# State space constants on VectorE in pieces, and half of the block product's weight sums by adding transfers

## The chip, the cores and the metric

The kernel runs on one core of a Trainium2 chip. The core has TensorE (PE: matmuls, 128 rows by up to 512 columns), VectorE (DVE) and ScalarE (ACT) for elementwise work, GpSimd (POOL), SyncE (SP) and DMA queues that SP, ACT and POOL issue to. Each engine runs its own list of instructions in order and waits for the others by semaphores. The metric is the device time of one execution in microseconds (us); lower is better.

## The reference

One layer of a hybrid decoder block on x of 512 tokens by 1024 features, all in float32:

```python
h = h + 0.5 * swiglu(rmsnorm(h, norm_ffn1), ffn1_w1, ffn1_w3, ffn1_w2)   # d_ff 2816
z = rmsnorm(h, norm_mix) @ w_in           # attention q, k, v, gates, and u for S5
h = h + concat([o_nsa, o_s5]) @ w_out
h = h + 0.5 * swiglu(rmsnorm(h, norm_ffn2), ffn2_w1, ffn2_w3, ffn2_w2)
h = h + sigmoid(rmsnorm(h, norm_ple) @ w_ple_gate) * (p @ w_ple)
out = rmsnorm(h, norm_final)

def swiglu(x, w1, w3, w2):
    return (silu(x @ w1) * (x @ w3)) @ w2
```

The S5 mixer is a diagonal complex state space model of 32 groups with 64 states, 16 channels in and out. The kernel computes it with matrices built from the parameters: powers of the discretised transition (`pr`, `pi`) times the input and output matrices, and a table of cosines and sines of the state's angles (`tcs`). These constants depend on no token.

## The kernel before

**Layout and stages.** The activations lie transposed in SBUF as `h`, 128 partitions by 8 blocks by 512 tokens. In order run the first FFN (to some 412 us of the profile), the mixer (to 700), the second FFN (to 1062), and the gate and the last norm.

**Products.** All weights come as units of 128x1024 floats (512 KB), loaded into `raw`, a ring of four buffers (`load_unit`, L104 to 109). The loads are issued on ACT's queue. `split` (L142 to 150) makes two halves of reduced precision: ACT casts `hi` (L147), DVE subtracts `lo` (L149). Each product is three matmuls, hi by hi, hi by lo and lo by hi.

**FFN.** d_ff is cut into 22 tiles f of 128, in chunks 0-5, 6-11, 12-16, 17-21. `FFN_ORDER` makes the up product of the first tile of a chunk, then the down product of the chunk before it, then the other up tiles. A down product has 8 steps m; each is 18 (or 15) matmuls of 512 columns into `ps_C`, and DVE adds the result to `h` (L470).

An up tile f below `plain` takes 48 matmuls of 512 columns. The others are fast tiles: a block scheme of 7 products on quarters of the weights and of x (`begin`, `up_fast`), 84 matmuls of 256 columns in all. It needs sums of quarters of the weights. `prepare` makes them on two raw units r0 and r1, in place: four DVE operations of 128x512 (L344, L346, L347, L350), between which the units are split, and at last the split of the fourth sum into `ah` (ACT, L352) and `al` (DVE, L353). x's own combinations are made by `restate`, with four 128x1024 operations on POOL (L216 to L225). `plain` is 5 in the first FFN and 2 in the second.

**S5 constants.** `s5_constants` is a generator that the first FFN draws from. After an up tile f it is advanced as its yielded numbers say. DVE makes the small tables, POOL the large ones: `ft` (L670 to 672), `gt` (L687 to 689), `tcs` (L741 to 748). So that POOL does not start early, each block is issued after a small copy `seen` on POOL of a copy `step` on DVE from the tile just made (L503, L457). `turn_f` transposes `ft` on PE and stores `fs`; `make_m` makes `kt` on PE and stores it by 8 small transfers on SP's queue (L709), and `gt` by three. `fs`, `kt` and the table `w` share one buffer ("bx").

**Order.** A scheduler places each engine's instructions from the code's order and its own estimate of times; the buffers of the pools limit how far ahead it can put a load.

Of the kernel before, what the change touches and what calls it, by code (L numbers as in the profile page):

```python
# [76 lines left out]
def block_kernel(ctx: ExitStack, tc: tile.TileContext, a: dict, out: bass.AP):  # L77
# [53 lines left out]
    def unit(raw_only=False, keep=None, q=nc.scalar, after=None):  # L131
# [3 lines left out]
        if i not in raws:  # L135
            load_unit(i, q)
# [24 lines left out]
    class Norm:  # L161
# [34 lines left out]
        def restate(self, xs, t, pool):  # L196

            def row(k):
                return xs[k // 4][:, k % 4]

            def quarter(r, c):
                return xs[r][:, :, 256 * c:256 * c + 256]
# [8 lines left out]
            self.row = row  # L211
            for k in range(KT):
                V.scalar_tensor_tensor(row(k), h[:, k, :], gains[:, self.gi, k:k + 1], self.rb, OP.mult, OP.mult)  # L213
# [5 lines left out]
            G.tensor_tensor(t, t, quarter(1, 1), OP.subtract)  # L219
            yield  # L220
            self.t2 = held(2)
            G.tensor_tensor(t, t, quarter(1, 0), OP.add)
            yield
            self.t4 = held(4)
            G.tensor_tensor(quarter(0, 1), quarter(0, 1), quarter(1, 1), OP.subtract)  # L225
# [3 lines left out]
        def resplit(self, k):  # L229
            S.copy(self.xh[:, k], self.row(k))  # L230
            V.tensor_tensor(self.xl[:, k], self.row(k), self.xh[:, k].bitcast(F32), OP.subtract)

# [91 lines left out]
    def ffn(nrm, done, plain, xp, hp, fp, bg=None, first=None, restate=None):  # L324
        wait = next(bg) if bg else None
        fast = not bg
        if True:
            hid = {}

            def hidden(f, t3):  # L330
                hq = hp.tile([128, 2, SEQ], FR, tag="hq", name="hq")
                hh, hl = hq[:, 0], hq[:, 1]
                if fast or f >= plain:
                    S.copy(hh, t3)  # L334
                else:
                    V.tensor_copy(hh, t3)
# [3 lines left out]
            def prepare(f):  # L340

                r0, r1 = unit(True), unit(True)
                a0, a1 = (r.rearrange("p (b c) -> p b c", b=2) for r in (r0, r1))
                V.tensor_tensor(a0[:, 1], a0[:, 0], a0[:, 1], OP.add)  # L344
# [5 lines left out]
                V.tensor_tensor(a1[:, 1], a0[:, 1], a1[:, 1], OP.add)  # L350
# [38 lines left out]
            def up_fast(f, after):  # L389
# [12 lines left out]
                t1 = fp.tile([128, SEQ], F32, tag="t1", name="t1")  # L402
# [14 lines left out]
            def up(f):  # L417
# [21 lines left out]
                t1 = fp.tile([128, SEQ], F32, tag="t1", name="t1")  # L439
# [14 lines left out]
            def step(f):  # L454
                if bg and wait is not None:
                    state["step"] = pace.tile([128, 1], F32, tag="step", name="step", bufs=3)
                    V.tensor_copy(state["step"], hid[f][1][:, 0:1].bitcast(F32))  # L457

            def down(fl, last):
                n = len(fl)  # L460
                cur = None
                for m in range(KT):
# [7 lines left out]
                    V.scalar_tensor_tensor(h[:, m, :], o, 0.5, h[:, m, :], OP.mult, OP.add)  # L470
                    if last:
                        done(m)
                    elif m == KT - 2:
                        for _ in begin(fl[-1] + 2):
                            pass

            for kind, i in FFN_ORDER:
                if kind == "up":
                    up(i)
                    step(i)  # L480
                    for _ in range(4):
                        if wait is not None and i >= wait:
                            wait = next(bg, None)
# [13 lines left out]
    def s5_constants(sp):  # L497
        yield 6
        if True:
            def paced():  # L500

                seen = sp.tile([128, 1], F32, tag="seen", name="seen")
                return tc.issue_after(G.tensor_copy(seen, state["step"]).ins)  # L503

# [3 lines left out]
            def late(dst, src):  # L508
                with tc.issue_after(loads[7].ins):
                    nc.scalar.dma_start(dst, src)  # L510
# [43 lines left out]
            yield 1  # L554
# [6 lines left out]
            yield 1  # L561

            J = 9
# [4 lines left out]
            for j in range(1, J):  # L568
                V.tensor_scalar(ph[:, j], ph[:, 0], float(2 ** j), None, OP.mult)
            yield 1  # L570
# [7 lines left out]
            yield 1  # L578
# [5 lines left out]
            yield 1  # L584
# [5 lines left out]
            yield 1  # L590

            pr, pi = t32("pr", 9), t32("pi", 9)
            u1, u2 = t32("u1", 4), t32("u2", 4)
# [16 lines left out]
            yield 1  # L610
# [15 lines left out]
            yield 1  # L626
# [16 lines left out]
            yield 1  # L643
# [19 lines left out]
            def big(c, n, name):  # L663
                t = sp.tile([128, 8, n, 16], F32, tag=f"big{c % 2}", name=name)
                return t, sp.tile([128, 8, n, 16], F32, tag="bt", name="bt")

            def make_f(c):
                ft, bt = fts[c], _ = big(c, 8, "ft")
                with paced():
                    G.tensor_tensor(*spread(ft, b2[:, 0, chunk(c)], pr[:, 0:8, chunk(c)]))  # L670
                    G.tensor_tensor(*spread(bt, b2[:, 1, chunk(c)], pi[:, 0:8, chunk(c)]))
                    G.tensor_tensor(ft, ft, bt, OP.add)
# [11 lines left out]
            def make_g(c):  # L684
                gt, bt = gts[c], _ = big(c, 9, "gt")
                with paced():
                    G.tensor_tensor(*spread(gt, cx[:, 0, chunk(c)], pr[:, :, chunk(c)]))  # L687
                    G.tensor_tensor(*spread(bt, cx[:, 1, chunk(c)], pi[:, :, chunk(c)]))
                    G.tensor_tensor(gt, gt, bt, OP.subtract)
# [4 lines left out]

            def make_m(c):
                kt = sp.tile([16, 8, 128], F32, tag="bx", name="kt")
                p = bank("C")
                for n in range(8):
                    j, i = n // 4, n % 4
                    mm(p[32 * j:32 * j + 16, i * 128:(i + 1) * 128], b2[:, 0, 8 * c + n, :],  # L700
                       gts[c][:, n, 0:8].rearrange("p k o -> p (k o)"), True, True)
# [10 lines left out]
            for i in range(10):  # L712
                yield 7 + i
# [894 lines left out]
```

## Time and profile before

| | us |
|---|---|
| median of 3 runs | 1123.72 |
| lowest, highest | 1117.9, 1126.02 |
| the profiled execution | 1124.48 |
| its span | 1122.7 |
| mean clock of PE granted | 0.978 of full speed |
| busy POOL in the span | 180.1 |

The profile is of one execution, of which 1.8 us lie outside the span. Its views used below: the page's shares and the chain that ended last (followed back from the last instruction to what released it); busy times by stretch of the span; the groups of instructions of a line and shape with their count, total and mean; the chain of waits in a stretch in order of time; and the transfers with their size and the median time from issue to landing. PE's matmuls overlap in the records, so the mean length of a record is longer than the time between two.

### The profile page before, as it was taken

The page shows a single profiled execution, that of the slowest core. Times are in us where ns is not written, and L with a number is a line of the kernel's source. Part 1 is how long each engine was busy: PE and PEld are TensorE (multiplying, and loading weights), DVE is VectorE, ACT ScalarE, POOL GpSimd, SP SyncE. Part 2 cuts the span into 40 slices and gives each one's busy share as a digit, 9 for nine tenths or more (in the row PEclk, how much of TensorE's full clock was granted, in tenths as well). Part 3 has the DMA queues.
Part 4 walks back from the last instruction along what each step waited for, and adds up shares of the span by engine and source line. Part 5 has one row for each costly group of instructions (what it writes and reads, how often), then busy time and mean ns, then how long its engine had stood idle before and what let it go on. Part 6 is the DMA issues. An engine that isn't in the chain of part 4 may idle for free.

```text
span 1122.7 us, 16766 instructions
## 1 busy us (share of the span) xinstructions
PE 1054.2 (94%) x6518; PEld 908.0 (81%) x6518; DVE 847.6 (75%) x1362; ACT 518.3 (46%) x918; POOL 180.1 (16%) x174
## 2 busy tenths in 40 slices
PE   6989997999899899989799999999999999999996
PEld 5778897889789778867457667699899899898895
DVE  6899889868657796689548896887578658666776
ACT  5344253425424442345736894655245335245541
POOL 5210027623432982010000000000000000000000
PEclk9999998999999999999989999999999999999998
DMA  8314222643632557885522002324323313324402
GB/s 257 117 38 151 75 76 88 209 116 86 182 95 76 169 138 243 231 264 155 178 85 76 1 20 71 135 76 123 104 75 114 132 57 113 132 76 151 148 22 75
DMA packets 76543, 132.78 MB, mean 118 GB/s; under 512 B 26528, under 2 KB 45984, under 8 KB 76464
## 3 DMA queue, kind: packets, MB, share of 16 engines
q10 hardware_dynamic: 26080, 90.51, 25.7%
q1 hardware_dynamic: 47312, 29.89, 9.6%
q0 software_dynamic: 3072, 11.31, 3.1%
q8 instruction: 51, 0.84, 0.3%
q14 instruction: 28, 0.23, 0.1%
HBM read 114.09 MB, written 17.83 MB: 118 GB/s over the span
## 4 chain that ended last, share of the span: by engine, by line
PE 70%; DVE 12%; issue 6%; ACT 6%; DMA 4%; SPq 1%; ACTq 0%; DVEq 0%; POOLq 0%; POOL 0%
PE ps_C L126 22%; PE ps_B L126 19%; PE ps_A L126 19%; PE ps_D L126 11%; DVE lo L149 4%; DMA raw<-in_wpack 2%; DMA qf<-qd 1%; ACT e L850 1%; ACT hi L147 1%; SPq L709 1%; ACT eh L850 1%; ACT ps_B L850 1%; DVE t L414 1%; DVE xn L213 1%; DVE hq L337 1%
## 5 line engine op out<-in xcount | busy, mean ns | idle before, releaser
L149 DVE TENSOR_TENSOR lo<-raw,hi 128x1024 fp32r<-128x1024 f32 (+2 forms) x203 | 270.4, 1358 | 70.8 <-ACT hi L147 68.7
L147 ACT CAST hi<-raw 128x1024 fp32r<-128x1024 f32 (+2 forms) x203 | 207.6, 1041 | 244.3 <-PE ps_C L126 91.7
L126 PE MATMUL ps_C<-hq,hi 128*128 128x512 f32 x704 | 219.2, 393 | 4.0 <-ACT hq L334 2.3
L126 PEld LDWEIGHTS ps_C<-hq,hi 128*128 128x128 f32 x704 | 131.0, 189 | 33.4 <-DVE h L470 3.2
L126 PE MATMUL ps_A<-xh,lo 128*128 128x256 f32 (+1 forms) x456 | 140.3, 308 | 7.1 <-DVE lo L149 7.1
L126 PE MATMUL ps_A<-xh,hi 128*128 128x256 f32 (+1 forms) x456 | 139.8, 309 | 7.1 <-ACT xh L170 6.4
L126 PE MATMUL ps_A<-xl,hi 128*128 128x256 f32 (+1 forms) x456 | 140.9, 311 | 2.5 <-DVE xl L171 1.1
L126 PE MATMUL ps_C<-hq,lo 128*128 128x512 f32 x352 | 136.6, 391 | 0.0
L302 POOL TENSOR_TENSOR ri<-ms,negh 128x4 f32<-128x4 f32 (+1 forms) x6 | 7.4, 1226 | 589.6 <-DVE ms L301 589.5
L126 PEld LDWEIGHTS ps_A<-xh,lo 128*128 128x128 f32 x456 | 87.2, 191 | 11.8 <-DVE lo L149 8.2
L126 PEld LDWEIGHTS ps_A<-xh,hi 128*128 128x128 f32 x456 | 87.0, 192 | 11.7 <-ACT xh L170 6.4
L126 PEld LDWEIGHTS ps_A<-xl,hi 128*128 128x128 f32 x456 | 87.0, 192 | 11.1 <-DVE xl L171 3.9
L126 PE MATMUL ps_B<-sh,hi 128*128 128x256 f32 x296 | 86.5, 292 | 7.1 <-ACT pu L365 4.9
L126 PE MATMUL ps_B<-sl,hi 128*128 128x256 f32 x296 | 85.4, 288 | 0.0
L126 PE MATMUL ps_B<-sh,lo 128*128 128x256 f32 x296 | 85.0, 287 | 0.0
L126 PEld LDWEIGHTS ps_C<-hq,lo 128*128 128x128 f32 x352 | 66.4, 189 | 13.8
L126 PE MATMUL ps_D<-sh,lo 128*128 128x256 f32 x228 | 64.2, 282 | 2.2 <-DVE lo L149 2.2
L126 PEld LDWEIGHTS ps_B<-sh,hi 128*128 128x128 f32 x296 | 58.2, 197 | 9.4 <-ACT pu L365 5.5
L126 PE MATMUL ps_D<-sh,hi 128*128 128x256 f32 x228 | 63.9, 282 | 0.4 <-ACT hi L147 0.4
L126 PE MATMUL ps_D<-sl,hi 128*128 128x256 f32 x228 | 63.6, 281 | 0.0
L126 PEld LDWEIGHTS ps_B<-sl,hi 128*128 128x128 f32 x296 | 58.2, 196 | 0.2
L126 PEld LDWEIGHTS ps_B<-sh,lo 128*128 128x128 f32 x296 | 58.3, 197 | 0.0
(407 smaller groups left out, 2469.0 us busy)
## 6 DMA issues: line engine op xcount, KB each, us to landing
raw<-in_wpack ACTq DMA_DIRECT2D x168, 512.0 KB, 3.7
so<-s5o POOLq DMA_DIRECT2D x8, 768.0 KB, 6.3
si<-s5i POOLq DMA_DIRECT2D x8, 512.0 KB, 6.6
raw<-in_wpack SPq DMA_DIRECT2D x4, 512.0 KB, 6.6
h<-in_xT SPq DMA_DIRECT2D x8, 256.0 KB, 5.3
s5i<-fs SPq DMA_DIRECT2D x4, 512.0 KB, 3.9
s5o<-gt SPq DMA_DIRECT2D x4, 512.0 KB, 3.3
s5o<-gt SPq DMA_DIRECT2D x8, 256.0 KB, 4.6
```

The costliest lines, as they stand in the source:

```text
L126: return PE.matmul(o, lhsT, rhs, start=start, stop=stop, **kw)
L147: S.copy(hi[:, c], raw[:, c])
L149: V.tensor_tensor(lo[:, c], raw[:, c], hi[:, c].bitcast(F32), OP.subtract)
L213: V.scalar_tensor_tensor(row(k), h[:, k, :], gains[:, self.gi, k:k + 1], self.rb, OP.mult, OP.mult)
L302: G.tensor_tensor(ri, ms, negh[:, :nb], OP.pow)
L337: V.tensor_tensor(hl, t3, hh.bitcast(F32), OP.subtract)
L414: V.tensor_tensor(t3, t1, t3, OP.mult)
L709: nc.sync.dma_start(md[16 * (7 - e):16 * (7 - e) + 16, chunk(c), 16 * e:], kt[:, :, :128 - 16 * e])
L850: S.activation(*args, **kw)
```

## The change

**S5 constants.** `ft`, `gt` and `tcs` are made by DVE. `rotated` makes each of `ft` and `gt` in three operations and yields after each; `tcs` is rewritten as four operations on both halves at a time for each doubling, where six were. `step`, `seen` and `paced` are gone. The new `aside(n, mark)` advances the generator n times, with the pieces issued after the instruction `mark`: behind the h-update of each step of a down product (2 pieces for even m, 1 for odd m, in the first chunk from m = 5), three pieces after the up tiles 4, 5 and 6, and one after each from 8 on.

**Weight sums.** In `prepare` the first sum is an accumulating transfer on POOL's queue that reads the quarter again from DRAM (L362 of the new kernel), and the fourth one from SBUF to SBUF (L368). Each moves 128x512 floats. The second and third sum stay on DVE (L364, L365).

**Raw units.** While `more` is set, every fifth unit in the first FFN lies in a fifth buffer, and in the second FFN there are eight; the loads go to SP's queue, not ACT's.

**Others.** `PLAIN1` is 7, not 5. `restate` runs on DVE, in 128x512 pieces, and its input lies in other buffers (`Rows`). `hidden` always copies on ACT. `t1` has one buffer in the first FFN. S5 parameters are loaded on SP's queue.

```diff
+    more = []
     def load_unit(i, q):
         w = UNIT_W[i]
-        raw = ring.tile([128, UNIT], F32, tag="raw", name="raw", bufs=4)
+        if more and i % (4 + more[1]) >= 4:
+            raw = more[0].tile([128, UNIT], F32, tag="raw", name="raw", bufs=more[1])
+        else:
+            raw = ring.tile([128, UNIT], F32, tag="raw", name="raw", bufs=4)
...
         if i not in raws:
-            load_unit(i, q)
+            load_unit(i, q or (nc.sync if more else nc.scalar))
...
-            G.tensor_tensor(t, quarter(0, 1), quarter(0, 0), OP.subtract)
+            combine(tq, quarter(0, 1), quarter(0, 0), OP.subtract)
...
             def prepare(f):
+                i = unit_i[0]
                 r0, r1 = unit(True), unit(True)
                 a0, a1 = (r.rearrange("p (b c) -> p b c", b=2) for r in (r0, r1))
-                V.tensor_tensor(a0[:, 1], a0[:, 0], a0[:, 1], OP.add)
+                src = a["wpack"][128 * UNIT_OFF[i]:128 * UNIT_OFF[i + 1]].rearrange("(p c) -> p c", c=UNIT)
+                nc.gpsimd.dma_start(a0[:, 1], src[:, 0:512], accum_op=OP.add)
                 yield split(r0)
                 V.tensor_tensor(a0[:, 1], a0[:, 1], a1[:, 0], OP.add)
                 V.tensor_tensor(a0[:, 0], a0[:, 0], a0[:, 1], OP.subtract)
                 yield split(r0)
                 yield split(r1)
-                V.tensor_tensor(a1[:, 1], a0[:, 1], a1[:, 1], OP.add)
+                nc.gpsimd.dma_start(a1[:, 1], a0[:, 1], accum_op=OP.add)
...
-            def step(f):
-                if bg and wait is not None:
-                    state["step"] = pace.tile([128, 1], F32, tag="step", name="step", bufs=3)
-                    V.tensor_copy(state["step"], hid[f][1][:, 0:1].bitcast(F32))
+            def aside(n, mark=None):
+                for _ in range(n if bg else 0):
+                    with tc.issue_after(mark.ins) if mark else nullcontext():
+                        next(bg, None)
...
-                    V.scalar_tensor_tensor(h[:, m, :], o, 0.5, h[:, m, :], OP.mult, OP.add)
+                    mark = V.scalar_tensor_tensor(h[:, m, :], o, 0.5, h[:, m, :], OP.mult, OP.add)
...
+                    if not last:
+                        aside((2 - m % 2) * (m > 4 or fl[0] > 0), mark)
...
                     up(i)
-                    step(i)
-                    for _ in range(4):
-                        if wait is not None and i >= wait:
-                            wait = next(bg, None)
+                    aside(SMALL.get(i, int(i > 7)))
...
-            def make_f(c):
-                ft, bt = fts[c], _ = big(c, 8, "ft")
-                with paced():
-                    G.tensor_tensor(*spread(ft, b2[:, 0, chunk(c)], pr[:, 0:8, chunk(c)]))
-                    G.tensor_tensor(*spread(bt, b2[:, 1, chunk(c)], pi[:, 0:8, chunk(c)]))
-                    G.tensor_tensor(ft, ft, bt, OP.add)
+            def rotated(kept, c, n, name, x, y, sub):
+                t = kept[c] = sp.tile([128, 8, n, 16], F32, tag=f"big{c % 2}", name=name)
+                u = sp.tile([128, 8, n, 16], F32, tag="bt", name="bt")
+                V.tensor_tensor(*spread(t, x[:, chunk(c)], pr[:, 0:n, chunk(c)]))
+                yield
+                V.tensor_tensor(*spread(u, y[:, chunk(c)], pi[:, 0:n, chunk(c)]))
+                yield
+                V.tensor_tensor(t, t, u, sub)
+                yield
...
-                        G.tensor_tensor(t, si, bi, OP.mult)
-                        G.tensor_tensor(dr, sr, br, OP.mult)
-                        G.tensor_tensor(dr, dr, t, OP.subtract)
-                        G.tensor_tensor(t, si, br, OP.mult)
-                        G.tensor_tensor(di, sr, bi, OP.mult)
-                        G.tensor_tensor(di, di, t, OP.add)
+                    V.tensor_tensor(t[:, 0], old[:, 1], angle(nsn, 1), OP.mult)
+                    V.tensor_tensor(t[:, 1], old[:, 0], angle(sn, 1), OP.mult)
+                    V.tensor_tensor(new, old, angle(cs, 2), OP.mult)
+                    V.tensor_tensor(new, new, t, OP.add)
...
+    more[:] = fp2, 4
     ffn(n2, feed_next(3), N_PLAIN, x2pool, hp2, fp2)
+    del more[:]
...
-PLAIN1 = 5
+PLAIN1 = 7
+SMALL = {4: 3, 5: 3, 6: 3}
```

**How the order of instructions moves.** First DVE in the second FFN, one steady fast tile, before (t: the tile's product, p and pu: copies of partial sums):

```order
L149 TENSOR_TENSOR lo<-raw,hi 128x1024 x3
L350 TENSOR_TENSOR raw<-raw 128x512
L414 TENSOR_TENSOR t_7996<-t_7995,t_7996 128x512
L346 TENSOR_TENSOR raw<-raw 128x512
L353 TENSOR_TENSOR al<-raw,ah 128x512
L404 TENSOR_TENSOR t_8121<-ps_D,pu 128x256
L347 TENSOR_TENSOR raw<-raw 128x512
L337 TENSOR_TENSOR hq<-t_7996,hq 128x512
L344 TENSOR_TENSOR raw<-raw 128x512
L408 TENSOR_TENSOR t_8121<-p_8065,ps_B 128x256
```

The same cycle of DVE after:

```order
L154 TENSOR_TENSOR lo<-raw,hi 128x1024 x3
L432 TENSOR_TENSOR t_7661<-t_7660,t_7661 128x512
L364 TENSOR_TENSOR raw<-raw 128x512
L365 TENSOR_TENSOR raw<-raw 128x512
L353 TENSOR_TENSOR hq<-t_7661,hq 128x512
L422 TENSOR_TENSOR t_7786<-ps_D,pu 128x256
L371 TENSOR_TENSOR al<-raw,ah 128x512
L426 TENSOR_TENSOR t_7786<-p_7730,ps_B 128x256
```

Two of the four sums are gone from the cycle (L344 and L350 before); `al` (L371) now reads what the transfer of L368 has written.

In the first FFN POOL's list before, in the middle of the constants:

```order
L503 COPY seen<-step 128x1
L687 TENSOR_TENSOR gt<-cx,pr 128x1152
L688 TENSOR_TENSOR bt<-cx,pi 128x1152
L689 TENSOR_TENSOR gt<-gt,bt 128x1152
L503 COPY seen<-step 128x1
```

DVE's list after, where the second down product begins (h is its update):

```order
L488 SCALAR_TENSOR_TENSOR h<-ps_C,h 128x512
L678 TENSOR_TENSOR ft<-b_862,pr 128x1024
L680 TENSOR_TENSOR bt<-b_862,pi 128x1024
L432 TENSOR_TENSOR t_1824<-t_1823,t_1824 128x512
L154 TENSOR_TENSOR lo<-raw,hi 128x1024
L353 TENSOR_TENSOR hq<-t_1824,hq 128x512
L488 SCALAR_TENSOR_TENSOR h<-ps_C,h 128x512
L682 TENSOR_TENSOR ft<-ft,bt 128x1024
```

The products have left POOL and stand between DVE's updates of h, one or two behind each.

POOL at the end of the mixer and the start of the second FFN, after (L908 loads an S5 constant, L322 is the norm's power):

```order
L908 DMA so<-s5o 128x1536 x2
L362 DMA raw<-in_wpack 128x512 x2
L322 TENSOR_TENSOR ri<-ms,negh 128x4
L362 DMA raw<-in_wpack 128x512 x2
L368 DMA raw<-raw 128x512
```

Before, the power (L302) stood right behind the last load of S5; now two adding transfers stand between them.

SP's queue in the first FFN, after:

```order
L714 DMA s5o<-kt 16x8x16
L111 DMA raw<-in_wpack 128x1024
L698 DMA s5o<-gt 128x8x128
L700 DMA s5o<-gt 64x8x128 x2
L111 DMA raw<-in_wpack 128x1024
L698 DMA s5o<-gt 128x8x128
L700 DMA s5o<-gt 64x8x128 x2
L714 DMA s5o<-kt 16x8x128
```

The loads of weights, which stood on ACT's queue, now stand between the stores of `gt` and `kt`.

More of the change, by code (lines that the diff above doesn't have):

```diff
@@ L194, in quarter, with restate @@
             return self.xh[:, ks, cs], self.xl[:, ks, cs]
[L196 to L202, printed above, removed]
+        def restate(self, rows, t, pool):
+            self.row = lambda k: rows[k]
             def held(n):
@@ L231, in resplit, with __init__, pair, __getitem__ @@
             V.tensor_tensor(self.xl[:, k], self.row(k), self.xh[:, k].bitcast(F32), OP.subtract)
+    class Rows:
+        def __init__(self, tiles):
+            self.pairs = [tiles[0][:, 0:2], tiles[0][:, 2:4], *tiles[1:]]
+        def pair(self, k):
+            return self.pairs[k // 2]
+        def __getitem__(self, k):
+            return self.pairs[k // 2][:, k % 2]
     class Scaled(Norm):
@@ L332, in hidden @@
                 hh, hl = hq[:, 0], hq[:, 1]
[L333 to L336, printed above, removed]
+                S.copy(hh, t3)
                 V.tensor_tensor(hl, t3, hh.bitcast(F32), OP.subtract)
@@ L438, in up @@
                     nrm.finish()
[L439 removed]
+                t1 = fp.tile([128, SEQ], F32, tag="t1", name="t1", bufs=2 if fast else 1)
                 t3 = fp.tile([128, SEQ], F32, tag="t3", name="t3")
@@ L682, in turn_f, with make_m @@
                 nc.sync.dma_start(fd[:, chunk(c)], fs)
[L684 to L689, printed above, removed]
+            def make_m(c):
+                gt = gts[c]
                 ko = gt[:, :, 1:9, :].rearrange("p g k o -> p g (k o)")
@@ L711, in s5_constants @@
             fts, gts = {}, {}
-            for i in range(10):
-                yield 7 + i
-                if 2 <= i < 6:
-                    turn_f(i - 2)
-                if i >= 6:
-                    make_m(i - 6)
-                if i < 4:
-                    make_f(i)
-                elif i < 8:
-                    make_g(i - 4)
+            late_ = []
+            for kept, n, name, x, y, sub, then in ((fts, 8, "ft", b2[:, 0], b2[:, 1], OP.add, turn_f),
+                                                   (gts, 9, "gt", cx[:, 0], cx[:, 1], OP.subtract, make_m)):
+                for c in range(4):
+                    for i, _ in enumerate(rotated(kept, c, n, name, x, y, sub)):
+                        if i == 1 and late_:
+                            late_.pop()()
+                        yield
+                    late_.append(lambda then=then, c=c: then(c))
@@ L747, in s5_constants, with angle @@
-                nc.sync.dma_start(cd[:, gs_], tc_)
-                G.tensor_scalar(ts_, ts_, pos, None, OP.mult)
-                nc.sync.dma_start(sd[:, gs_], ts_)
+                    def angle(t, m):
+                        t = t[:, 1 + j, gs_]
+                        if m > 1:
+                            return t[:, None, :, None].to_broadcast([128, m, 16, n])
+                        return t[:, :, None].to_broadcast([128, 16, n])
+                    old, new, t = tcs[:, :, :, 0:n], tcs[:, :, :, n:2 * n], w1[:, :, :, 0:n]
@@ L752, in block_kernel @@
+                V.tensor_scalar(tcs[:, 1], tcs[:, 1], pos, None, OP.mult)
+                nc.sync.dma_start(sd[:, gs_], tcs[:, 1])
+                yield
     state = {}
@@ L767, in block_kernel @@
         bg = s5_constants(sp)
-        xs = [sp.tile([128, 4, SEQ], F32, tag=f"big{i}", name="xn") for i in range(2)]
         xt = sp.tile([128, 4, 256], F32, tag="bt", name="xt")
-        for k in range(KT):
-            n1.square(k, G, xs[k // 4][:, k % 4])
         with (tc.tile_pool(name="xpool1", bufs=1, reuse_waits="tile") as x1,
@@ L774, in block_kernel @@
             pad(x1, XSHIFT)
-            parts = n1.restate(xs, xt, x1)
             with tc.tile_pool(name="hid", bufs=7, reuse_waits="tile") as hp1:
                 hp1.tile([128, (512 - XSHIFT) // 4], F32, name="pad", bufs=1)
-                ffn(n1, feed_next(1), PLAIN1, x1, hp1, fp1, bg, first, parts)
+                rows = Rows([sp.tile([128, 4, SEQ], F32, tag="big0", name="xn")] +
+                            [hp1.tile([128, 2, SEQ], F32, tag="hq", name="xn") for _ in range(2)])
+                for k in range(KT):
+                    n1.square(k, G, rows[k])
+                more[:] = fp1, 1
+                ffn(n1, feed_next(1), PLAIN1, x1, hp1, fp1, bg, first, n1.restate(rows, xt, x1))
+                del more[:]
         for _ in bg:
```

88 lines of the change are left out of this document (44 added, 44 removed).

## The prediction

> **What bounds the kernel now.** I read the page first, from the top. TensorE (PE) is busy 94% of the span, and the chain that ended last is 70% PE. So nearly three quarters of the time is matmul, and what a change of this kind can win is the rest of that chain: VectorE (DVE) 12%, ACT 6%, issue 6%, DMA 4%.
>
> ```profile
> span 1122.7 us, 16766 instructions
> PE 1054.2 (94%) x6518; PEld 908.0 (81%) x6518; DVE 847.6 (75%) x1362; ACT 518.3 (46%) x918; POOL 180.1 (16%) x174
> PE 70%; DVE 12%; issue 6%; ACT 6%; DMA 4%; SPq 1%; ACTq 0%; DVEq 0%; POOLq 0%; POOL 0%
> ```
>
> Shares are means over unlike stages, so I cut the span into stretches next: the first FFN (to 412 us), the mixer (412 to 700), the second FFN (700 to 1062), the rest. The columns are the stretch, its length, busy time of PE, its weight loads, DVE, ACT and GpSimd (POOL), then clock, DMA share, GB/s.
>
> ```profile
> 60.00:106.00 46.00, 41.56 (x249) 36.59 (x248) 45.73 (x108) 22.29 (x34) 2.40 (x1) 0.96 0.28 88
> 142.00:210.00 68.00, 58.53 (x450) 57.25 (x449) 61.65 (x62) 33.53 (x60) 34.58 (x18) 0.92 0.33 102
> 260.00:310.00 50.00, 43.84 (x348) 40.44 (x348) 37.05 (x51) 24.18 (x42) 23.05 (x12) 0.96 0.56 158
> 370.00:412.00 42.00, 37.36 (x191) 31.14 (x190) 35.39 (x37) 18.27 (x29) 40.70 (x50) 0.96 0.56 162
> 700.00:742.00 42.00, 39.44 (x193) 31.28 (x192) 35.20 (x53) 24.66 (x35) 1.03 (x1) 1.00 0.31 102
> 742.00:1030.00 288.00, 288.00 (x2046) 271.05 (x2045) 203.08 (x273) 129.66 (x210) 0.00 (x0) 1.00 0.34 106
> ```
>
> The last row is the yardstick. From 742 to 1030 PE never stops, and POOL does nothing. In the first FFN the same tiles run, but POOL is at work for the S5 constants, and PE has holes in exactly the stretches where POOL is busy: 142 to 210, 260 to 310, 370 to 412.
>
> What an unbroken PE does is in the chain of waits of the second FFN (start, length, what, number of instructions): a down product's 512-column matmul takes 23.14/102 = 0.227 us. A fast up tile starts its like piece at 845.32 and again at 855.25, so a tile lasts 9.93 us; its 84 matmuls of 256 columns take 0.118 us each.
>
> ```profile
> 791.81 23.14 PE ps_C L126 x102
> 845.32 1.91 PE ps_A L126 x16
> 855.25 1.91 PE ps_A L126 x16
> ```
>
> Now the stretch of the first FFN from 106.2 us (end of the first plain tiles) to 412, 305.8 us. The groups of PE by shape there:
>
> ```profile
> L126 PE MATMUL ps_C<-hq,hi 128*128 128x512 f32 x324 | 102.2, 396 | 2.5 <-ACT hq L334 1.2 <-DVE h L470 0.9 <-ACT fs L681 0.3
> L126 PE MATMUL ps_C<-hq,lo 128*128 128x512 f32 x163 | 63.8, 393 | 0.0
> L126 PE MATMUL ps_B<-sh,hi 128*128 128x256 f32 x120 | 36.6, 305 | 4.9 <-ACT pu L365 4.9
> L126 PE MATMUL ps_C<-gt,b 128*16 128x128 f32 x64 | 6.9, 274 | 0.7 <-POOL gt L689 0.7
> ```
>
> There are 324 + 163 = 487 down matmuls: 110.6 us. The 120 of the third row are 8 in each of 15 fast tiles (f = 7 to 21): 15 x 9.93 = 149.0 us. The S5 products are the 64 of the last row and 32 transposes, about 10 us. That makes 270 of 305.8, so some 35 us are lost there. By the same count with a cut at each stretch I get 15.5 us lost from 142 to 210, 9.8 from 260 to 310, 7.7 from 370 to 412, 2 in between. These 35 us are what the change can win.
>
> Why they are lost: DVE's rows by shape, from 142 to 210, from 210 to 410 and from 742 to 1060.
>
> ```profile
> L149 DVE TENSOR_TENSOR lo<-raw,hi 128x1024 fp32r<-128x1024 f32 x16 | 33.2, 2118 | 2.7 <-ACT hi L147 2.7
> L350 DVE TENSOR_TENSOR raw<-raw 128x512 f32<-128x512 f32 x5 | 7.0, 1397 | 0.0
> ...
> L149 DVE TENSOR_TENSOR lo<-raw,hi 128x1024 fp32r<-128x1024 f32 x43 | 65.7, 1554 | 17.4 <-ACT hi L147 17.3
> ...
> L149 DVE TENSOR_TENSOR lo<-raw,hi 128x1024 fp32r<-128x1024 f32 x79 | 93.7, 1222 | 37.1 <-ACT hi L147 35.3 <-PE ps_C L126 1.7
> L353 DVE TENSOR_TENSOR al<-raw,ah 128x512 fp32r<-128x512 f32 x20 | 13.8, 688 | 2.2 <-ACT ah L352 1.8
> L350 DVE TENSOR_TENSOR raw<-raw 128x512 f32<-128x512 f32 x19 | 13.1, 687 | 0.1
> ```
>
> The same subtraction takes 2118 ns beside POOL and 1222 ns without it; the sum of L350 takes 1397 against 687. So a POOL product does not lie beside DVE's work, it stretches it. A fast tile costs DVE three lo (3.67), four sums (2.75), three more of 128x512 (2.06) and two of 128x256 (0.84): 9.3 of PE's 9.93 us without POOL. Any stretching makes DVE the bound.
>
> From 260 to 310 there is a second cause: the chain runs through SP's queue and the small transfers of kt, whose one buffer must be empty before ACT writes the next kt ahead of its casts.
>
> ```profile
> 279.66 2.89 SPq L709
> 285.58 1.52 DMA s5o<-kt
> 301.86 3.17 DMA s5o<-kt
> 306.20 0.61 ACT hq L334
> ```
>
> **The change, part by part.**
>
> *S5 products from POOL to DVE.* POOL's groups that go, and a DVE product with a broadcast operand for their price:
>
> ```profile
> L689 POOL TENSOR_TENSOR gt<-gt,bt 128x1152 f32<-128x1152 f32 x4 | 14.3, 3584 | 0.3
> L672 POOL TENSOR_TENSOR ft<-ft,bt 128x1024 f32<-128x1024 f32 x4 | 11.2, 2797 | 0.2
> L503 POOL COPY seen<-step 128x1 f32<-128x1 f32 x20 | 13.0, 649 | 204.2 <-DVE step L457 204.2
> L636 DVE TENSOR_TENSOR b<-bx,qr x1: 684/684/684, 116.8 to 116.8; 128x512 f32<-128x512 f32 x1
> ```
>
> A broadcast product of 128x512 takes DVE 684 ns, as much as L350, so 128x1024 takes 1.22 (the lo row) and 128x1152 about 1.37. Twelve of each are 31 us; the twiddles (tcs), rewritten in wide operations, write 12,096 elements in each partition, about 16 us at the lo row's 1.2 ns. DVE so takes on some 47 us. In return the stretching goes: of lo alone 16 x 0.90 + 43 x 0.33 = 28.5 us, with the sums and products of 128x512 about 42. POOL's paced copies (seen) go with the 20 small step copies on DVE. The two nearly cancel as totals; what changes is the place. Most pieces stand behind down products, where 18 matmuls (4.1 us) of PE ask DVE for a lo and an h-update (about 1.9 us).
>
> *Two of the four sums by adding transfers.* In each of 35 fast tiles (15 and 20) two sums of 0.69 us leave DVE: a fast tile falls from 9.3 to 7.9 us. In the second FFN that wins nothing, because PE is full there already (row 742 to 1030). In the first it pays for the pieces that fall into up tiles.
>
> The price is latency, and the trace has no adding transfer. The second sum (L368 of the new kernel) may start only when the lo of r1 is read; its result must be copied on ACT and subtracted on DVE (0.61 in the last row above, 0.69) before PE's products with ah. Between lie five half products of 12 matmuls, 60 x 0.118 = 7.1 us. So 7.1 - 1.3 = 5.8 us are free, and about 1 us more where DVE runs ahead: a limit near 6.8. The nearest rows (KB each, median us from issue to landing):
>
> ```profile
> raw<-in_wpack ACTq DMA_DIRECT2D x168, 512.0 KB, 3.7
> si<-s5i POOLq DMA_DIRECT2D x8, 512.0 KB, 6.6
> rope<-in_rope POOLq DMA_DIRECT2D x2, 256.0 KB, 3.4
> pled<-et SPq DMA_DIRECT2D x8, 256.0 KB, 2.0
> L893 POOL DMA_DIRECT2D si<-s5i x8 | 4.4, 548 | 67.1 <-PE ps_C L126 48.6 <-DVE z L911 18.2 <-issue 0.3
> ```
>
> The bounds are 2.0 us (a plain store of 256 KB) and 6.6 (512 KB on POOL's queue, since an add reads its target too). I take 5, nearer to the POOL rows, and hence no stall on PE; the cover is those 60 matmuls. The Trainium skill ("DMA: Bandwidth & Descriptors", Anatomy of one DMA — SWDGE (gpsimd) path) gives a transfer from POOL's queue about 2.0 us and its bytes at 436 GB/s. By it a 256 KB sum would be an estimated 2.6 us, and the sum below would be the same with more room; rope's 3.4 is already above it.
>
> *POOL's queue.* At the start of the second FFN two adding transfers stand ahead of the norm's power on POOL (L322), on which the start of that FFN hangs. Issuing costs 0.55 us each, and they wait for raw loads (3.7 us): 0 to 4.8 us. I take 2, as the loads are issued early.
>
> *Loads on SP, more raw units.* ACT no longer issues loads. In the first FFN they now queue on SP with gt's and kt's transfers, where a kt waits for its copy; five units instead of four are the cover. The kt chain (three rows above) stays, so I leave 4 of the 9.8 us of 260 to 310.
>
> *Plain tiles 5 to 7, restate on DVE.* A plain tile is 48 x 0.227 = 10.9 us against 9.93: two are +1.9 us. Eight sums of 128x512 come to DVE (5.5 us) before the first down product, where DVE is full (45.73 of 46). In return two tiles ask it for two lo and not for 9.3 us of fast work. I call the start even, with 4 us either way. The mixer's own steps are not touched; I count nothing there.
>
> **The sum.** Of the 35 us there remain 2.5 of 15.5, 4 of 9.8, 4 of 7.7 (end of the last chunk, where DVE also makes squares), 2: 12.5. Then -22.5 + 1.9 + 2 = -18.6. The profiled execution took 1124.5 us, so 1105.9; the median of the runs is 0.8 lower, so 1105.
>
> **The rivals.**
>
> *Adding transfers come late: slower.* For: the POOL rows reach 6.6, and POOL's queue is in order, so a sum can stand behind another transfer that still waits for its load. Against: the second FFN's DMA share is 0.34, there is room. Each us above 6.8 costs up to 35 us over 35 tiles. At 8 us: 1105 + 42 = 1147; it decides against the change from 7.4 us on (35 x 0.6 = 21). Chance 0.17. The skill ("SBUF — State Buffer", SBUF: two separate sides) has a rule that would make this likelier: VectorE operations in a two-port mode keep GpSimd from writing descriptors. The new DVE order of a fast tile holds hardly any such operation, and no run here shows one beside an adding transfer.
>
> *DVE or SP's queue stays the bound in the first FFN: no change.* After 106 us I count DVE's unstretched work as 217 us against some 255 of PE, but in up tiles 13 to 21 it is about 95% of PE's time. If the lost time stays at 25 of 35: 1123.7 - 10 + 3.9 = 1117, range 1113 to 1123. Chance 0.20.
>
> *Nearly all is recovered,* also what is lost before 106 us (DVE 45.73 of 46): 1123.7 - 33 = 1091 and down to 1086. Chance 0.10.
>
> *The stretching is not POOL's doing.* Then DVE only gets 47 us more and 21 less (30 sums), and most of the 26 land on the path, since DVE has no room in up tiles: about 1140. Against it: DMA share and GB/s are alike in 142 to 210 and 742 to 1030, POOL is the difference. Chance 0.03.
>
> **The numbers.** The forecast (1096 to 1112) has 0.50. A measurement of this kernel tells about 1% from no change. Below 1112.5 lie the forecast and the full recovery, 0.60; within 1% the bound that stays and late transfers of a small size, 0.23; above 1135 the rest, 0.17. The range for 8 in 10 reaches from 1088 to 1134, with nearly all of the no-change case and the mildest late transfers; the forecast's own range is 1096 to 1112.
>
> **What would show it.** Right: lo near 1222 ns all through the first FFN; POOL busy below 20 us there; PE without holes in 142 to 210; adding transfers at 4 to 6 us from issue to landing; the second FFN still at 288 us for that row. Wrong: PE in the second FFN waiting for al or ah (late transfers); ACT waiting for raw with SP's queue as releaser; DVE above 95% in up tiles 13 to 21 with PE waiting for lo; ri of the second FFN's norm waiting on POOL's queue.

## The result and the profile after

| | before | after |
|---|---|---|
| median, us | 1123.26 | 1096.11 |
| lowest, highest, us | 1117.9, 1126.02 | 1091.53, 1096.64 |
| the profiled execution, us | 1124.48 | 1096.0 |
| ratio to before | | 0.9755, 95% interval 0.971 to 0.98 |

The changed kernel is 2.4% faster. The forecast was 1105, with 1096 to 1112 as its own range and 1088 to 1134 as the range for 8 in 10. The time lies 0.1 us above the lower end of the first.

The page of the changed kernel, with its span, the engines' busy time and the chain that ended last:

```profile
span 1094.2 us, 16835 instructions
PE 1042.1 (95%) x6446; PEld 897.5 (82%) x6446; DVE 794.0 (73%) x1339; ACT 516.8 (47%) x911; POOL 92.7 (8%) x118
PE 62%; ACT 4%; issue 3%; DVE 3%; DMA 3%; ACTq 0%; SPq 0%; POOLq 0%; POOL 0%; DVEq 0%
```

DVE has gone from 847.6 to 794.0 us. The shares of this chain add up to 75% only: the walk back breaks off at 263.8 us, so they leave out most of the first FFN, and DVE's 3% can't be set against the 12% of the chain before. PE has 72 matmuls fewer, as each of the two plain tiles has 48 in place of 84. The stretches that the prediction cut out, in the changed kernel (stretch, length, PE, its weight loads, DVE, ACT, POOL, clock, DMA share, GB/s):

```profile
60.00:106.00 46.00, 45.04 (x199) 36.95 (x198) 43.49 (x125) 18.14 (x25) 1.00 (x2) 1.00 0.35 98
142.00:210.00 68.00, 67.28 (x485) 62.97 (x484) 49.57 (x64) 33.38 (x56) 6.95 (x8) 1.00 0.68 181
260.00:310.00 50.00, 46.81 (x283) 42.22 (x282) 36.98 (x59) 19.17 (x29) 4.32 (x5) 0.97 0.65 165
742.00:1030.00 288.00, 286.26 (x1926) 263.87 (x1925) 178.79 (x234) 126.86 (x202) 26.87 (x32) 1.00 0.50 131
```

From 142 to 210 PE rose from 58.53 to 67.28 of 68 us, DVE fell from 61.65 to 49.57, and the granted clock rose from 0.92 to 1.00. The groups of DVE from 100 to 400 show why:

```profile
L154 DVE TENSOR_TENSOR lo<-raw,hi 128x1024 fp32r<-128x1024 f32 x69 | 82.8, 1222 | 18.1 <-ACT hi L152 17.2 <-issue 0.4
L680 DVE TENSOR_TENSOR bt<-cx,pi 128x1152 f32<-128x1152 f32 x4 | 5.4, 1352 | 0.0
L678 DVE TENSOR_TENSOR ft<-b,pr 128x1024 f32<-128x1024 f32 x4 | 4.9, 1218 | 0.0
```

No lo is stretched any more. Before, its mean here was 2118 ns up to 210 us and 1554 after that; now it is 1222, as in the second FFN. The S5 products cost DVE 1.22 and 1.35 us, against 2.8 and 3.6 of their slowest on POOL.

To compare the stages of many runs I use one measure, the loss of PE: over all pairs of successive matmuls, the time from start to start less the unbroken time of the first (0.227 us for 512 columns, 0.1185 for 256, 0.1 for 128). The four stages are cut at the first and last down matmul of the first FFN and, for the second, at the first product with ah and the last down matmul. The end, 8 to 9 us in all runs, is left out. The few matmuls of other sizes stand mostly in the mixer; what is taken for them moves its whole column by about 1 us and not the differences. The measure counts a matmul that runs slowly as it counts a wait, so time at a lower granted clock is in it.

| loss of PE in us | start | rest of first FFN | mixer | second FFN |
|---|---|---|---|---|
| before | 17.6 | 35.3 | 39.9 | 2.1 |
| after | 6.8 | 13.7 | 42.3 | 2.2 |
| sums_on_dve | 6.7 | 8.4 | 43.6 | 2.2 |
| sums_on_dve_ffn2 | 6.6 | 14.5 | 43.9 | 2.7 |
| s5_on_pool_sums_on_dve | 6.8 | 46.4 | 46.9 | 2.1 |
| s5_on_pool | 6.7 | 34.2 | 43.3 | 2.1 |
| four_units_act | 6.7 | 20.9 | 41.6 | 14.6 |
| plain_5 | 7.7 | 12.9 | 38.8 | 2.1 |
| restate_on_pool | 7.0 | 18.2 | 41.3 | 3.8 |
| fourth_sum_in_two | 6.7 | 20.8 | 40.8 | 4.7 |
| pieces_in_ups_sums_on_dve | 6.7 | 19.0 | 43.2 | 2.2 |
| pieces_in_ups | 6.7 | 16.8 | 42.1 | 2.1 |
| sums_dve_four_units_plain_5 | 8.8 | 9.4 | 39.5 | 2.1 |
| also_restate_on_pool | 16.0 | 8.4 | 40.1 | 2.1 |

From before to after the two parts of the first FFN lose 10.8 + 21.6 = 32.4 us less, the mixer 2.4 more; two plain tiles add 1.9. That is the gain of 28.5 us between the two spans, to 0.4 us. The table is of one execution each; the medians below are the surer evidence.

Part of the gain in the rest of the first FFN comes by way of the granted clock. Two rows of the kernel before, the end of a wait of PE and what follows it (columns as above):

```profile
190.00:193.30 3.30, 0.81 (x7) 0.68 (x6) 3.30 (x3) 0.28 (x2) 1.49 (x1) 1.00 0.51 159
193.30:196.70 3.40, 3.40 (x18) 3.40 (x17) 2.68 (x6) 1.77 (x4) 0.99 (x2) 0.50 0.56 127
```

In the second row PE is busy throughout, but the clock is at 0.50, and its matmuls of 256 columns start 0.21 us apart instead of 0.1185. In this stage the clock was at half for 20.5 us before and for 3.4 after. By the count above the matmuls that only ran more slowly lost 7.7 of the 35.3 us before and 1.5 of the 13.7 after. The slow stretches come with long waits. In this stage PE has 16 waits above 2.5 us in the 14 traces of this document (four before, of 2.7 to 4.9 us, and one after, of 2.9), and at 15 of them the clock fell to half before the wait ended or within 2 us after it. In the four kernels where PE has no wait above 1.6 us there (plain_5, sums_on_dve, sums_dve_four_units_plain_5, also_restate_on_pool) it stayed full. So this time is counted here as a cost of the waits, although no run sets the clock by itself.

### The profile page after: what moved, and what is told of

It is laid out like the page before. It is cut to its first block, busy times and chain, and to the rows that moved or that the text cites. A ratio compares the mean times of both kernels' runs of the same rounds, so it can differ in the third digit from the quotient of the medians.

```text
span 1094.2 us, 16835 instructions
## 1 busy us (share of the span) xinstructions
PE 1042.1 (95%) x6446; PEld 897.5 (82%) x6446; DVE 794.0 (73%) x1339; ACT 516.8 (47%) x911; POOL 92.7 (8%) x118
## 3 DMA queue, kind: packets, MB, share of 16 engines
q0 software_dynamic: 13152, 29.66, 13.7%
## 4 chain that ended last, share of the span: by engine, by line
PE 62%; ACT 4%; issue 3%; DVE 3%; DMA 3%; ACTq 0%; SPq 0%; POOLq 0%; POOL 0%; DVEq 0%
PE ps_A L131 18%; PE ps_C L131 18%; PE ps_B L131 17%; PE ps_D L131 10%; DMA qf<-qd 2%; ACT e L863 1%; ACT eh L863 1%; ACT ps_B L863 1%; DMA raw<-in_wpack 1%; DVE el L1264 0%; DVE lo L154 0%; ACT hi L152 0%; DMA qd<-r 0%; ACT QA L1149 0%; ACT pt L1270 0%
## 5 line engine op out<-in xcount | busy, mean ns | idle before, releaser
L154 DVE TENSOR_TENSOR lo<-raw,hi 128x1024 fp32r<-128x1024 f32 (+2 forms) x201 | 240.0, 1218 | 70.8 <-ACT hi L152 66.4
L131 PE MATMUL ps_B<-sh,hi 128*128 128x256 f32 x280 | 79.1, 283 | 2.7 <-ACT ps_B L399 2.7
L131 PE MATMUL ps_B<-sh,lo 128*128 128x256 f32 x280 | 78.8, 281 | 0.7 <-DVE lo L154 0.7
L131 PE MATMUL ps_B<-sl,hi 128*128 128x256 f32 x280 | 78.9, 282 | 0.0
L362 POOL DMA_DIRECT2D raw<-in_wpack x35 | 30.4, 869 | 483.7 <-DVE h L1127 168.3
L488 DVE SCALAR_TENSOR_TENSOR h<-ps_C,h 128x512 f32<-128x512 f32 x64 | 43.9, 689 | 36.8 <-PE ps_C L131 36.4
L131 PE MATMUL ps_D<-sh,lo 128*128 128x256 f32 x220 | 61.7, 281 | 0.0
L131 PE MATMUL ps_D<-sl,hi 128*128 128x256 f32 x220 | 61.3, 281 | 0.0
L131 PE MATMUL ps_B<-xh,hi 128*128 128x512 f32 (+1 forms) x164 | 57.9, 353 | 0.9 <-ACT hi L152 0.9
L131 PE MATMUL ps_B<-xh,lo 128*128 128x512 f32 (+1 forms) x160 | 56.0, 350 | 0.8 <-DVE lo L154 0.8
```

Of the source, the lines that this page charges most:

```text
L131: return PE.matmul(o, lhsT, rhs, start=start, stop=stop, **kw)
L154: V.tensor_tensor(lo[:, c], raw[:, c], hi[:, c].bitcast(F32), OP.subtract)
L362: nc.gpsimd.dma_start(a0[:, 1], src[:, 0:512], accum_op=OP.add)
L488: mark = V.scalar_tensor_tensor(h[:, m, :], o, 0.5, h[:, m, :], OP.mult, OP.add)
```

## The experiments

Each kernel is the changed one with the edit shown. Ratios are to the kernel before on the same chip.

### The four sums on DVE again

```diff
-                nc.gpsimd.dma_start(a0[:, 1], src[:, 0:512], accum_op=OP.add)
+                V.tensor_tensor(a0[:, 1], a0[:, 0], a0[:, 1], OP.add)
...
-                nc.gpsimd.dma_start(a1[:, 1], a0[:, 1], accum_op=OP.add)
+                V.tensor_tensor(a1[:, 1], a0[:, 1], a1[:, 1], OP.add)
```

> All four sums of the weight quarters are DVE operations again in both FFNs, everything else as changed. Theory A (the transfers pay for the S5 pieces: DVE has no room in the up tiles of the first FFN with 9.3 us of its own work per 9.93 us tile): the first FFN loses 8 to 15 us more, 1104 to 1111 us. Rival B (the move of the S5 products alone does it, the transfers are idle): within 3 us of the changed kernel's 1096.

Measured: 1092.34, ratio 0.9746 (0.9711 to 0.9781). Theory A falls. What rival B says holds, though the median lies 0.7 us below its range: without its transfers the kernel is no slower than with them. The medians differ by 3.8 us the other way, the ratios by 0.1%, which the intervals do not separate. The loss table puts the difference in the rest of the first FFN, 8.4 us against 13.7. Where the transfers cost time there is in the waits of the changed kernel from 240 to 266 (who waited for whom, us, times, longest), and in the timeline of POOL and ACT:

```profile
ACT ah L370 <- DMA raw<-raw: 10.1, 2, 5.2
PE ps_B L131 <- ACT ps_B L399: 2.7, 1, 2.7
```

```profile
255.45 0.86 POOL L362 DMA_DIRECT2D raw<-in_wpack  x1 [11.19 <-DVE lo L154]
255.99 1.22 POOL L368 DMA_DIRECT2D raw<-raw  x1
...
262.20 0.62 ACT L370 CAST ah<-raw 128x512 fp32r<-128x512 f32 x1 [5.20 <-DMA raw<-raw]
262.73 1.04 ACT L152 CAST hi<-raw 128x1024 fp32r<-128x1024 f32 x1
263.67 0.36 ACT L399 COPY ps_B<-ps_A 128x256 f32<-128x256 f32 x1
```

A first sum (L362) of a later tile goes out just ahead of the fourth sum (L368). The fourth then takes until 262.2, and ACT stands at ah for 5.2 us, the longer of the two waits in the first row. Of the 35 fourth sums, the five that went out less than 2 us behind a first sum took 4.7 to 7.3 us to land, and the median of the others is 3.3. It is an in-order engine: the cast and the copy behind ah need nothing of the transfer, but PE waits 2.7 us for that copy, and from 266.0 to 269.5 the clock is at half. With the sums on DVE the rows from 260 to 310 of the two kernels differ as follows (the changed kernel's stands above):

```profile
260.00:310.00 50.00, 50.00 (x314) 45.20 (x313) 43.47 (x80) 19.77 (x31) 0.00 (x0) 1.00 0.41 117
```

DVE is busier there, 43.47 against 36.98 us, and PE has no hole.

### The sums on DVE in the second FFN alone

The same edit, under `if fast`.

> The sums are DVE operations again in the second FFN only. Theory A (the second FFN was full before and the transfers win nothing there): 1096, within 2 us. Rival B (the transfers gave the start of the second FFN its 1 us, or cost POOL's queue something): 1098 or more, or 1094 or less.

Measured: 1097.22, ratio 0.9782 (0.9749 to 0.9814). Theory A holds: in the second FFN the transfers win nothing and cost nothing (2.7 us of loss without them, 2.2 with them).

### The S5 products on POOL, with and without the transfers

```diff
-                V.tensor_tensor(*spread(t, x[:, chunk(c)], pr[:, 0:n, chunk(c)]))
+                G.tensor_tensor(*spread(t, x[:, chunk(c)], pr[:, 0:n, chunk(c)]))
```

and so on in `rotated` and for `tcs`; the first run has the sums on DVE as above too.

> The S5 products are back on POOL at their new places, and all four sums are on DVE; the other parts of the change stay. Theory A (POOL's products stretch DVE's work): lo beside them is near 2 us again, the first FFN loses some 25 us more than in the changed kernel, 1115 to 1125. Rival B (the places, the two more plain tiles and the fifth unit made the gain): 1100 to 1106.

> The S5 products are back on POOL at their new places, the adding transfers stay on POOL's queue behind them. Theory A (stretched DVE work, and transfers that wait for products of 2.5 to 3.5 us in POOL's order): 1108 to 1125. Rival B (two sums fewer per tile give DVE the room, the stretching then costs nothing): within 4 us of 1096.

Measured: 1129.34, ratio 1.007 (1.0037 to 1.0103), and 1114.62, ratio 0.9942 (0.9917 to 0.9966). What theory A says holds in both, though the first lies 4 us beyond its range. With all else equal, the move of the S5 products alone is worth 1129.3 - 1092.3 = 37 us at their new places. The first run is slower than the kernel before, so these 37 us are not this move's share of the 27 us that were gained. DVE's lo in 100 to 370, first with the sums on DVE, then with the transfers:

```profile
L154 DVE TENSOR_TENSOR lo<-raw,hi 128x1024 fp32r<-128x1024 f32 x57 | 88.4, 1581 | 9.8 <-ACT hi L152 9.8
...
L154 DVE TENSOR_TENSOR lo<-raw,hi 128x1024 fp32r<-128x1024 f32 x60 | 88.7, 1510 | 13.2 <-ACT hi L152 13.1
```

The stretching is back in both, 1581 and 1510 against 1221 and 1220 without POOL's products. So it is POOL's doing, and the rival that denied this falls. Nor does PE wait for the slower products themselves: from 90 to 418 us of the first run its listed waits add up to 29.1 us, 23.3 of them for results of DVE and none for POOL. The Trainium skill ("SBUF — State Buffer", Who interferes with whom) says that a VectorE instruction with two SBUF inputs contends with a GpSimd instruction that reads SBUF; these four numbers agree. Only here do the transfers pay: 1129.3 - 1114.6 = 14.7 us, 12.2 of it in the rest of the first FFN by the table. The likely reason is that DVE's work is stretched and two sums less per tile shorten it, although a fourth sum may come late. The chain of waits of the second run:

```profile
354.84 0.16 issue
355.00 1.23 DVE lo L154
356.23 0.29 issue
356.52 7.35 DMA raw<-raw
```

Here the fourth sum takes 7.35 us to land, twice the median of 3.5 us of this run, and lies on the path.

### Four raw units, loads on ACT's queue

```diff
-                more[:] = fp1, 1
...
-    more[:] = fp2, 4
```

> No further raw buffers, and the loads are on ACT's queue as before; the rest is as changed. Theory A (four units are few for a first sum that needs the load and then a transfer of 4.2 us ahead of the split): PE waits for lo and hi in both FFNs, 1102 to 1125. Rival B (loads were early enough anyway): within 3 us of 1096.

Measured: 1113.44, ratio 0.9931 (0.99 to 0.9962). Theory A holds. The second FFN loses 14.6 us, not 2.2. Its chain of waits there:

```profile
828.24 0.70 DVE t L432
828.97 3.48 DMA raw<-in_wpack
832.98 5.27 DMA raw<-in_wpack
838.28 1.05 ACT hi L152
839.67 0.82 issue
840.50 0.69 DVE t L432
841.22 3.43 DMA raw<-in_wpack
845.21 4.37 DMA raw<-in_wpack
849.60 1.05 ACT hi L152
```

Both transfers of a pair are on the path, the unit's load and then the first sum, which is a transfer into the same buffer; only after both may ACT cast hi. Both bear the same name; by the issues ACT's queue sends the load at 828.97 and POOL the sum at 832.98. Both loads were issued 0.01 us after ACT began the copy hq, before which it had stood 1.07 and 1.34 us for DVE's t. So each stood behind that wait in ACT's list. Whether its buffer was free sooner, and what the four buffers cost apart from the queue, this run does not show.

### Five plain tiles

```diff
-PLAIN1 = 7
+PLAIN1 = 5
```

> Five plain tiles in place of seven. Theory A (DVE was the bound ahead of the first down product, and the two plain tiles are why the start got 8 us shorter): the start falls back by 4 to 8 us, less 1.9 us for the two tiles: 1098 to 1103. Rival B (the start got shorter by restate on DVE and the thinner small pieces): 1094, 2 us less than the changed kernel.

Measured: 1094.0, ratio 0.9768 (0.9736 to 0.9801). Theory A falls: the start loses 7.7 us with five plain tiles, 6.8 with seven. The median is that of rival B, 2.1 us below the changed kernel, but the ratios differ by 0.1% the other way, so the price of two plain tiles is not measured here.

### restate on POOL

```diff
-                    V.tensor_tensor(dst(i), x(i), y(i), op)
+                    G.tensor_tensor(dst(i), x(i), y(i), op)
```

> The four combinations of x are on POOL again (in 128x512 pieces). Theory A (POOL's operations are slow and stretch DVE, and the start hangs on them): 1098 to 1102. Rival B (they lie beside other work): within 2 us of 1096.

Measured: 1098.25, ratio 0.9797 (0.9763 to 0.983). Inconclusive: the median lies just beyond rival B's range, at the lower edge of theory A's, and the intervals of the two kernels overlap. The start loses 7.0 us, as in the changed kernel, so theory A's reason (the start hangs on them) does not show. The traced execution loses more in the rest of the first FFN (18.2 against 13.7) and in the second (3.8 against 2.2); why stays open.

### The fourth sum by two transfers

```diff
-                nc.gpsimd.dma_start(a1[:, 1], a0[:, 1], accum_op=OP.add)
+                sc = xp.tile([128, 512], F32, tag="sc", name="sc", bufs=1)
+                nc.gpsimd.dma_start(sc, a0[:, 1])
+                nc.gpsimd.dma_start(a1[:, 1], sc, accum_op=OP.add)
```

> The fourth sum takes two transfers in a row: one copies the quarter to a scratch tile, the next adds the scratch tile. That doubles its latency to 7 or 8 us, where the prediction put the limit at 6.8. Theory A (limit 6.8): PE waits for al in the second FFN too, 0.3 to 1.5 us in each of 35 tiles, 1106 to 1150. Rival B (DVE and the queue run further ahead, so there is more room than the five half products): within 3 us of 1096.

Measured: 1105.91, ratio 0.9865 (0.9835 to 0.9895), 0.1 us below theory A's range and far above rival B's. But the run did not do what it was made for. POOL's timeline in the second FFN:

```profile
711.71 0.57 POOL L369 DMA_DIRECT2D sc<-raw  x1 [5.81 <-DVE raw L364]
716.71 0.86 POOL L370 DMA_DIRECT2D raw<-sc  x1 [4.43 <-DVE lo L154]
```

The copy to the scratch tile starts as soon as the sum on DVE (L364) is there, and the adding transfer later waits for lo, as it did without the copy. So the latency that counts was not doubled, and the second FFN lost only 2.5 us more. In the first FFN 7.1 us more are lost, with 15 more transfers on POOL's queue. Where late transfers begin to cost stays open.

### The pieces after the up tiles

```diff
-                    if not last:
-                        aside((2 - m % 2) * (m > 4 or fl[0] > 0), mark)
...
-                    aside(SMALL.get(i, int(i > 7)))
+                    aside(SMALL.get(i, 3 * int(i > 7)))
```

> The large S5 pieces are issued three after each up tile from 8 on and none behind the down products; all four sums are on DVE. Theory A (the place behind the down products is what lets DVE take the S5 products without the transfers): an up tile then asks DVE for 9.3 us and three pieces of 1.2 to 1.4 us against PE's 9.93, so 14 tiles lose up to 3 us each, less what runs ahead: 1105 to 1130. Rival B (DVE runs so far ahead that the place doesn't matter): within 3 us of the 1092 of sums_on_dve.

> The same places for the pieces, three after each up tile from 8 on, but with the adding transfers of the changed kernel. Theory A (the transfers pay only where DVE is the bound): an up tile asks DVE for 7.9 us and the pieces, 11.7 of 9.93, so it loses less than with the sums on DVE: 5 to 15 us below pieces_in_ups_sums_on_dve. Rival B (the transfers are never worth more than their waits): no faster than that run.

Measured: 1102.74, ratio 0.9841 (0.9815 to 0.9867), and 1102.45, ratio 0.9845 (0.9813 to 0.9878). The place is worth 10 us with the sums on DVE (1102.7 against 1092.3). That lies between the two ranges, nearer to theory A's; that DVE runs ahead in part is the likely reason. PE's longest wait from 90 to 391, with the sums on DVE, is at a DVE result:

```profile
PE ps_B L131 <- DVE t L426: 4.4, 1, 4.4
```

The second expectation's rival B holds: even with the pieces in the up tiles the transfers win 0.3 us, which is nothing.

### Three parts undone together, and restate too

The first kernel joins the edits of sums_on_dve, four_units_act and plain_5. The second adds that of restate_on_pool.

> Three parts of the change undone together: the four sums on DVE, four raw units with the loads on ACT's queue, five plain tiles. What stays is the move of the S5 products and of restate to DVE. Theory A (the further units only serve the transfers): the sum of sums_on_dve (-4) and plain_5 (-2): 1089 to 1093. Rival B (the further units also serve the first FFN's loads): 1096 to 1108.

> As sums_dve_four_units_plain_5 (1090), and the combinations of x are on POOL again too, so that of the change little more than the move of the S5 products to DVE stays. Theory A (in the kernel before, POOL's combinations and the stretching beside them caused most of the 11 us that the start lost more, and with five plain tiles nothing covers them): the start before the first down product loses 13 to 18 us, not 9; 1095 to 1100. Rival B (the start was long for other reasons, such as the casts on DVE and the S5 tables ahead): within 2 us of 1090.

Measured: 1090.11, ratio 0.9729 (0.9701 to 0.9757), and 1095.91, ratio 0.9757 (0.9741 to 0.9773). Theory A holds in both. The first has the lowest median of this study, and it has neither the transfers nor the further units: those units served the transfers. Its interval and the changed kernel's still overlap; its four times, 1088.7 to 1091.48, all lie below the changed kernel's 1091.53 to 1096.64. Its page:

```profile
span 1086.9 us, 16673 instructions
PE 1039.8 (96%) x6518; PEld 897.3 (83%) x6518; DVE 840.3 (77%) x1421; ACT 522.2 (48%) x923; POOL 32.6 (3%) x48
```

DVE is as busy there as before (847.6), and the span is 36 us shorter: the S5 products took about as much of DVE's time as the stretching had. The second kernel shows the start. Its chain of waits from 36 to 90 begins with DVE's scaling of x, and the groups of DVE from 30 to 100 give its mean, in this kernel and then in the first:

```profile
38.64 7.17 DVE xn L223 x6
```

```profile
L223 DVE SCALAR_TENSOR_TENSOR xn<-h,gains,rb 128x512 f32<-128x512 f32 x8 | 8.5, 1131 | 0.0
...
L223 DVE SCALAR_TENSOR_TENSOR xn<-h,gains,rb 128x512 f32<-128x512 f32 x8 | 5.4, 746 | 0.0
```

With POOL's combinations beside it the start loses 16.0 us, without them 8.8. With seven plain tiles it makes no difference (7.0 and 6.8), probably because the first fast tile then needs the combinations later. So in the changed kernel two parts cover the same loss, and either alone is enough.

## Why the prediction was right, and where its steps were not

**What bounds the kernel: right in the main.** In the stretches named (142 to 210, 260 to 310, 370 to 412) POOL's products stretched DVE's work, and the two runs with the products on POOL show that this is the cause. But the rest of the first FFN, where they lie, carries only 21.6 of the 32.4 us that this FFN lost less; the other 10.8 lie in the start. That PE has holes "in exactly the stretches where POOL is busy" was too strong: from 210 to 260 POOL was busy for 15.93 us and from 310 to 370 for 20.70, and PE for 49.70 of 50 and 60.00 of 60. A good part of both is down products, which ask little of DVE. And the clock column of those rows (0.92 and 0.96) was shown but not read.

**The sum for the rest of the first FFN: the total right to about 1 us, in part by luck.** 12.5 us were to remain, measured 13.7 (35.3 before, where the prediction had 35.0). Matched matmul by matmul, the three stretches of the prediction kept 0.3, 6.5 and 2.3 us, where 2.5, 4 and 4 were forecast, and the rest 4.6, where 2 were. The 4 us of 260 to 310 were left for the kt chain. With the sums on DVE the same matmuls lose nothing, so the 6.5 come with the transfers, and the kt chain was no longer a bound.

**The start: mis-sized.** "I call the start even, with 4 us either way" was the term that failed most. The start lost 10.8 us less. The prediction saw that DVE was full there (45.73 of 46), but counted the work to be added and not the stretching by POOL's combinations, which it had itself read off rows further on. In place of -18.6 the terms came to -21.6 - 10.8 + 1.9 + 2.4 = -28.1 us. The rival by which nearly all is recovered, also what is lost before 106 us, had this part right; its chance was put at 0.10. That the time still fell into the forecast's own range, by 0.1 us, is luck.

**Two plain tiles: not contradicted.** With the 1.9 us forecast the loss table closes to 0.4 us; the run with five could not measure them.

**POOL's queue at the second FFN's start: wrong.** Two microseconds were charged. POOL had issued both transfers by 671.8 us and then stood for DVE:

```profile
670.87 0.88 POOL L362 DMA_DIRECT2D raw<-in_wpack  x1 [9.59 <-DVE h L1127]
674.62 1.03 POOL L322 TENSOR_TENSOR ri<-ms,negh 128x4 f32<-128x4 f32 x1 [2.87 <-DVE ms L321]
```

So the transfers did not delay the norm's power.

**The mixer** was not counted; it lost 2.4 us more. Most of that lies at one place, the same 100 matmuls or so before and after:

```profile
495.00:509.00 14.00, 11.08 (x100) 8.55 (x100) 12.00 (x31) 5.89 (x15) 2.12 (x4) 1.00 1.07 319
465.00:485.00 20.00, 14.13 (x99) 10.82 (x98) 13.32 (x32) 6.45 (x16) 2.64 (x5) 0.74 0.84 235
```

They take 6 us longer, and the granted clock is at half for 10.2 us of them; other places give some 4 us back. Why the clock fell there these runs do not show.

**The transfers: the price was near, the purpose was wrong.** They land after 4.2 us (from DRAM) and 3.4 us (in SBUF), where 5 was taken. An issue costs POOL 0.87 us, not the 0.55 of a plain load that the prediction took:

```profile
L362 POOL DMA_DIRECT2D raw<-in_wpack x35 | 30.4, 869 | 483.7 <-DVE h L1127 168.3
...
raw<-in_wpack POOLq DMA_DIRECT2D x35, 256.0 KB, 4.2
raw<-raw POOLq DMA_DIRECT2D x35, 256.0 KB, 3.4
```

The 2.6 us by the Trainium skill's formula ("DMA: Bandwidth & Descriptors", Anatomy of one DMA — SWDGE (gpsimd) path) are below both; the measurement decides. The second FFN was not slowed, as forecast. But "in the first it pays for the pieces that fall into up tiles" did not hold: with all four sums on DVE the kernel is as fast or faster. The step that failed is the claim that a tile with 9.3 us of DVE work in 9.93 leaves no room. Down products leave DVE about half free, the pieces stand there (a place that is worth 10 us by itself), and DVE runs far enough ahead over a chunk. The mark of it foretold, POOL below 20 us in the first FFN, failed too: POOL was busy 47 us to 386 us, some 26 of them for the 30 issues of the transfers.

**The rival of late transfers** happened in a small way: one fourth sum behind a first sum in POOL's order, with ACT held for 5.2 us. The prediction had named that order and charged it to PE's wait for ah and al; what PE waited for was a copy behind ah on ACT.

## What to carry to other kernels

When one engine's work stretches another's, moving it to the engine that was stretched can leave that engine no busier: here DVE took 24 large products and the tables and was as busy as before in the best version. Place such work behind the products that ask little of the engine (here worth 10 us). And when a change has several parts, take each away by itself: of this one, the transfers and the further units that feed them gave nothing once the products had moved, and the units were needed only because of the transfers.

## What the hardware showed that was not expected

In the kernel before, two tiny DVE operations of 128x32 took 1.78 and 1.93 us, where the like one at 29.2 us took 0.18. POOL's and DVE's timelines from 54 to 65:

```profile
54.47 2.52 POOL L219 TENSOR_TENSOR xt<-xt,xn 128x1024 f32<-128x1024 f32 x1 [4.84 <-DVE sl L208]
61.60 2.40 POOL L222 TENSOR_TENSOR xt<-xt,xn 128x1024 f32<-128x1024 f32 x1 [4.61 <-DVE sl L208]
...
55.25 1.78 DVE L528 TENSOR_SCALAR ex<-x 128x32 f32<-128x32 f32 x1
62.10 1.93 DVE L530 TENSOR_SCALAR ex<-ex 128x32 f32<-128x32 f32 x1
...
54.65 0.68 DVE L445 TENSOR_TENSOR t<-ps_C,rb 128x512 f32<-128x512 f32 x1
```

POOL's operations end at 56.99 and 64.00, the two DVE operations at 57.03 and 64.03. Each of these two small operations ended with the large one on POOL that it had met, so its cost was what was left of POOL's operation and not its own length. It does not happen to every operation: L445, which reads ps_C from PSUM, ran beside the first of them in its usual 0.68 us.
